# A hybrid RWKV-7 and expert layer: an early gathered tile of 128 prompt tokens, and 544 instead of 672 tokens through all experts

## The chip, the cores and the metric

The kernel runs on one core of one Trainium2 chip. The metric is the device time of an execution in microseconds; lower is better. Before the change the median of three runs is 3515.53 us.

## The reference, cut to what matters

One layer is computed for 1024 prompt tokens and 32 sample tokens (8 sequences of 4), 1056 tokens in all, with a model width of 1024.

```python
def hybrid_layer(x, p, start_pos, shift_prev, wkv_prev, pool_prev, lw):
    n1 = rmsnorm(x, lw['norm_mix_g'])
    z = n1 @ lw['w_in']
    y_r, shift_new, wkv_new = rwkv7_mix(z[..., :D_SHIFT], ...)      # a scan over time with a matrix state
    y_p, pool_new = pool_mix(z[..., D_SHIFT:], pool_prev, ...)      # windowed means
    h = x + jnp.concatenate([y_r, y_p], axis=-1) @ lw['w_out']
    h = h + peer_ffn(rmsnorm(h, lw['norm_ffn_g']), lw['peer_wq'], lw['peer_keys'], lw['peer_u'], lw['peer_v'])
    gate = jax.nn.sigmoid(rmsnorm(h, lw['norm_ple_g']) @ lw['ple_gate_w'])
    h = h + (p @ lw['ple_w']) * gate
    return h, shift_new, wkv_new, pool_new

def block_fn(xb):                                    # of peer_ffn
    q = (xb @ wq).reshape(PEER_BLOCK, 8, 2, 128)
    s1, s2 = ...                                     # scores against two sets of 128 keys
    v1, i1 = lax.top_k(s1, 16); v2, i2 = lax.top_k(s2, 16)
    sc, ci = lax.top_k(all 256 sums v1 + v2, 16)
    expert = e1 * 128 + e2                           # 8 heads x 16 of 16384 experts per token
    gate = jax.nn.softmax(sc, axis=-1)
    ue = jnp.take(u_tab, expert, axis=0)
    act = gelu(einsum('thkd,td->thk', ue, xb)) * gate
    ve = jnp.take(v_tab, expert, axis=0)
    return einsum('thk,thkd->td', act, ve)
```

Each token so uses 128 of 16384 experts, each with a row of 1024 numbers in u and one in v. The outputs are the normed tokens and the new states, all in float32.

## The kernel before

Activations lie with the features on the 128 partitions and the tokens along the free dimension. Matmul operands are split into a high and a low part (hi, lo), and a product is three matmuls: hi by hi, hi by lo, lo by hi.

The instructions are written by a framework that orders them itself: it plays the program on a timeline, and at each moment an engine takes the ready instruction that stands earliest in the program text. The order within an engine is fixed at build time. Work that stands late in the text so fills gaps early, if its inputs and its memory are there. A pool of tiles (tile_pool) takes its memory when it is opened and gives it back when it is closed. DMAs are issued on the SP queue (nc.sync), the gathers on POOL's.

The stages in the text:

- **Phase A** (phase_a): the projections w_in of all 1056 tokens, the parts of RWKV that need no scan (written to fd), and the windowed means through pool_w (pmm, pdf; result yp_d). Each projection wmm also carries wsplit (L177 to L187): blocks of w_out and wq are loaded, split into hi and lo and stored to wc_d, by pieces of 256 KB, through single buffers sraw, shi and slo. For w_out only the first half of the rows is split.
- **Chunks** (bchunk): the scan over the prompt in 16 chunks of 64 tokens, each dependent on the state of the one before, and one chunk for the samples. The output goes to y_d. BC says which chunks are emitted with which stage.
- **ple and wpool** (L981, L998): p @ ple_w for all tokens, to pl_d; and x plus the pooled half of w_out for all tokens in slices of 352, to hx_d.
- **Phase C** (phase_c, one group of GROUPS at a time): y @ w_out (first half) + hx gives h (hT_d); the norm; 16 blocks of wq give the queries; their products with the keys are the scores (sc_d). Weights come from wc_d (wblock, L641); the last group splits its last blocks itself.
- **top and select** (L753, L772): for 128 tokens, on DVE, the 16 best of each half, of the sums, and the gates.

The experts are computed in two ways. Tokens in [GA, GB) are dense: for them select also writes the gates as one-hot products into g_d (L869 to L884), and all 16384 experts are computed in 128 blocks of 128: ublock (L1077: u, gelu), ugate (L1132: times the gate), vblock (L1145: v, eight ublocks at a time into OT). Each block streams 512 KB (esplit, L1057: eraw is split on ACT into ehi and on DVE into elo; upre does the first NPRE on POOL) and does 48 matmuls in emm (L1075) of ND/2 columns. The other GT tokens are gathered, in tiles of 128 (L1170 on): for each of 128 slots one indirect DMA on POOL (L1179) brings each token's own row of u (512 KB in all) into one of NROW = 4 buffers named row; one DVE instruction multiplies by the token and sums (L1187). After gelu and gate, 128 such gathers of v follow, each added to po on DVE (L1196). po is transposed on PE, added to h and stored in h2_d.

Tail (L1220 on) does the last gate, ple_gate_w, the sum and the final norm, once for the dense tokens (td) and once for the gathered ones (tg).

Lines that the text speaks of: keep and pconst (L106, L111), GROUPS and GA, GB (L40, L41), segs and tiles_of (L672, L678), merge (L919), the loop over steps (L1088 to L1118), the rows pool (L1125).

Of the kernel before, what the change touches and what calls it, by code (L numbers as in the profile page):

```python
# [19 lines left out]
D = 1024  # L20
KB = D // 128
NP = 1024
# [18 lines left out]
GROUPS = ((0, 288), (288, 544), (544, 800), (800, 1056))  # L41
GA, GB = 0, 672
# [19 lines left out]
def body(ctx, tc, io):  # L62
# [12 lines left out]
    hx_d = dram.tile([128, KB, T], F32, name="hx_d")  # L75
# [30 lines left out]
    keep = ctx.enter_context(tc.tile_pool(name="keep", bufs=1))  # L106
# [4 lines left out]
    pconst = phases.enter_context(tc.tile_pool(name="pconst", bufs=1))  # L111
# [8 lines left out]
    pbx = ExitStack()  # L120
# [44 lines left out]
    keys = pconst.tile([128, 2, 128], F32)  # L165
# [288 lines left out]

    maxn = max(b - a for a, b in GROUPS)
    def bchunk(c, sp=None):
# [7 lines left out]
        pos = 0 if smpl else NSMP + 64 * c  # L464
# [83 lines left out]
        def sample_s(k, o, last):  # L548
            for p in range(4):
                apb = sp[0][0].tile([128, NB, m], F32, name="apb", bufs=2)  # L550
# [42 lines left out]
        if smpl:  # L593
            po = out()
            for p in range(4):
                ps = PS(pst)
                for i, (k, s_) in enumerate(((1, vt), (0, u))):
                    uvb = sp_.tile([m, NB, 64], F32, name="uvb", bufs=2)
# [42 lines left out]
    def wblock(gi, b):  # L641
# [4 lines left out]
        for i in range(1 if b < KB else 2):  # L646
# [25 lines left out]
    def segs(gi):  # L672
        c0, c1 = GROUPS[gi]
        if c0 == 0:
            return ((0, NP, NSMP), (NSMP, 0, c1 - NSMP))
        return ((0, c0 - NSMP, c1 - c0),)
# [5 lines left out]
    def phase_c(gi):  # L682
# [14 lines left out]
        for k in range(HK):  # L697
            split(k, y[:, k, :n], yhi, ylo)
# [73 lines left out]
    def select(tk, col, m, V12, I12):  # L772
# [133 lines left out]

    def t_stream(gi):
        for t0, m in tiles_of(gi):
            if GA <= GROUPS[gi][0] + t0 < GB:
                yield from top(tk, GROUPS[gi][0] + t0, m)  # L910

    def t_len(gi):
        n = 0
        for t0, m in tiles_of(gi):
            if GA <= GROUPS[gi][0] + t0 < GB:
                n += 24 + m // 4
        return n
# [11 lines left out]
    BC = (0, 2, 4, 8, 12, 16)  # L929
# [23 lines left out]
    with tc.tile_pool(name="smp", bufs=1) as sp_, tc.tile_pool(name="hx", bufs=1) as hx:  # L953
# [17 lines left out]
        pT = sp_.tile([128, 2, T], F32, name="pT")  # L971
        nc.sync.dma_start(pT, io["p"])

        def split(pool, raw, shape, nm, bufs):
            hi = pool.tile(shape, F32R, name=nm + "hi", bufs=bufs)
            ACT(hi, raw, AF.Copy)
            lo = pool.tile(shape, F32R, name=nm + "lo", bufs=bufs)
            TT(lo, raw, hi.bitcast(F32), op=ALU.subtract)
            return hi, lo

        def ple():  # L981
            phi, plo = split(sp_, pT, [128, 2, T], "p", 1)
            for db in range(KB):
                wp = sp_.tile([128, 2, 128], F32, name="wp", bufs=2)
                nc.sync.dma_start(wp, io["ple_w"][db])
                hi, lo = split(sp_, wp, [128, 2, 128], "w", 2)
                pss = [PS("b3"), PS("b3"), PS("b2")]
                for k in range(2):
                    for w, x, first, last in ((hi, phi, k == 0, False), (hi, plo, False, False), (lo, phi, False, k == 1)):
                        for i, ps in enumerate(pss):  # L990
                            mm(ps[:, :XW], w[:, k, :], x[:, k, i * XW:(i + 1) * XW], start=first, stop=last)
                for i, ps in enumerate(pss):
                    o = sp_.tile([128, XW], F32, name="pout", bufs=2)
                    ACT(o, ps[:, :XW], AF.Copy)
                    nc.sync.dma_start(pl_d[:, db, i * XW:(i + 1) * XW], o)
                yield

        def wpool():  # L998
            yhi = hx.tile([128, PB, T], F32R, name="yhi")
            ylo = hx.tile([128, PB, T], F32R, name="ylo")  # L1000
            for g in range(PB):
                raw = hx.tile([128, T], F32, name="yraw", bufs=1)
                nc.sync.dma_start(raw, yp_d[:, g, :])
                ACT(yhi[:, g, :], raw, AF.Copy)
                TT(ylo[:, g, :], raw, yhi[:, g, :].bitcast(F32), op=ALU.subtract)
            for b in range(KB):
                raw = hx.tile([128, HK, 128], F32, name="wraw", bufs=2)
                nc.sync.dma_start(raw, io["w_out"][b, :, HK:, :])
                hi = hx.tile([128, HK, 128], F32R, name="whi", bufs=2)
                ACT(hi, raw, AF.Copy)  # L1010
                lo = hx.tile([128, HK, 128], F32R, name="wlo", bufs=2)
                TT(lo, raw, hi.bitcast(F32), op=ALU.subtract)
                for i in range(T // XW):
                    cs = slice(i * XW, (i + 1) * XW)
                    x = hx.tile([128, XW], F32, name="x", bufs=3)
                    nc.sync.dma_start(x, io["x"][:, b, cs])
                    ps = PS("b2")
# [361 lines left out]
```

## Time and profile before

| | us |
|---|---|
| runs shown | 3515.53, 3530.12, 3499.31 |
| median | 3515.53 |
| the profiled execution's own time | 3494.25 |
| its span, first to last instruction | 3492.4 |
| busy PE / DVE / POOL / ACT | 3262.7 / 2675.0 / 1769.3 / 1179.8 |
| first and last gather issued | 1499.8 and 3317.4 |

A row of a group names line, engine, operation, output and inputs, the shape and the count; behind the bar stand the busy time in us, the mean of one in ns, the idle time of the engine just before them, and what ended it. Consecutive matmuls overlap in the record, so their pace is read from one start to the next, not from the mean. In the windows each engine's busy time stands with its count of instructions in brackets, then the granted clock of TensorE, the DMA engines' busy share and GB/s.

### The profile page before, as it was taken

To read this page: it belongs to the slowest core of one execution; us is meant where nothing else is said; L and a number is where in the kernel's file an instruction comes from. 1 tells how busy PE (TensorE), PEld (TensorE's weight loads), DVE (VectorE), ACT (ScalarE), POOL (GpSimd) and SP (SyncE) were. 2 spreads that over 40 slices of the span, in tenths; PEclk is the share of its full clock that TensorE was granted. 3 is DMA by queue.
4 is the path that set the end of the run, shared out by engine and by line. 5 is a ranking of instruction groups with operands and counts; after the bars stand their busy time and mean duration, and the time that the engine had idled before them with its cause. 6 is when DMAs were issued, how large, how long until landed. Compare 5 with 4: busy or idle time off the path is not lost.

```text
span 3492.4 us, 57600 instructions
## 1 busy us (share of the span) xinstructions
PE 3262.7 (93%) x21831; PEld 3150.6 (90%) x21831; DVE 2675.0 (77%) x5366; ACT 1179.8 (34%) x1776; POOL 1769.3 (51%) x1433
## 2 busy tenths in 40 slices
PE   8997998999999899999999999999999999999997
PEld 7876998989989788999999999999999999999997
DVE  6767333279999799978788778878888787788866
ACT  6452424345556455322122122122122212222243
POOL 5434234145465454156656555555555565555635
PEclk9998999999999899999999999999999999999999
DMA  5667645767767867479888888889898898898834
GB/s 177 213 197 177 185 134 148 213 174 231 210 194 212 282 199 258 131 278 318 308 315 307 306 320 311 313 318 317 314 321 315 307 312 308 301 318 313 311 123 132
DMA packets 467861, 883.61 MB, mean 253 GB/s; under 512 B 129280, under 2 KB 252416, under 8 KB 463104
## 3 DMA queue, kind: packets, MB, share of 16 engines
q1 hardware_dynamic: 356992, 477.24, 43.5%
q0 software_dynamic: 110592, 402.70, 32.6%
q8 instruction: 171, 2.80, 0.3%
q14 instruction: 106, 0.87, 0.1%
HBM read 759.22 MB, written 120.60 MB: 252 GB/s over the span
## 4 chain that ended last, share of the span: by engine, by line
DMA 26%; PE 22%; DVE 19%; issue 14%; POOL 11%; ACT 1%; SPq 0%; POOLq 0%; DVEq 0%; ACTq 0%
DMA row<-v,idx 14%; POOL row L1179 10%; DMA row<-u,idx 7%; PE pd L1075 7%; PE ps L881 2%; DVE ab L875 2%; PE ps L663 2%; PE ps L661 2%; DVE row L1187 2%; PE ps L662 2%; DVE elo L1063 1%; DVE po L1196 1%; PE ps L526 1%; DVE ab L877 1%; DMA sraw<-wq 1%
## 5 line engine op out<-in xcount | busy, mean ns | idle before, releaser
L1179 POOL DMA_INDIRECT row<-u,idx x384 | 534.9, 1393 | 387.9 <-DVE row L1187 248.4
L1179 POOL DMA_INDIRECT row<-v,idx x384 | 520.5, 1355 | 377.3 <-DVE po L1196 222.4
L1196 DVE SCALAR_TENSOR_TENSOR po<-row,act,po 128x1024 f32<-128x1024 f32 x381 | 488.8, 1283 | 152.6 <-DMA row<-v,idx 147.8
L1187 DVE SCALAR_TENSOR_TENSOR row<-row,xt 128x1024 f32<-128x1024 f32 x384 | 463.6, 1222 | 179.4 <-DMA row<-u,idx 177.8
L1075 PE MATMUL pd<-XH,elo 128*128 128x336 f32 x2176 | 524.9, 323 | 52.2 <-DVE elo L1063 49.3
L1061 ACT ACTIVATE ehi<-eraw 128x1024 fp32r<-128x1024 f32 x278 | 293.0, 1054 | 750.3 <-PE pd L1075 676.1
L1075 PE MATMUL pd<-wh,elo 128*128 128x336 f32 (+1 forms) x2112 | 509.5, 320 | 31.2 <-DVE elo L1063 30.9
L1075 PE MATMUL pd<-XH,ehi 128*128 128x336 f32 x2176 | 518.0, 319 | 4.1 <-DVE OT L1150 2.3
L1075 PE MATMUL pd<-XL,ehi 128*128 128x336 f32 x2176 | 519.5, 320 | 0.0
L1075 PE MATMUL pd<-wh,ehi 128*128 128x336 f32 (+1 forms) x2112 | 506.5, 319 | 8.7 <-DVE tg L1260 6.3
L1075 PE MATMUL pd<-wl,ehi 128*128 128x336 f32 (+1 forms) x2112 | 504.3, 318 | 0.0
L1075 PEld LDWEIGHTS pd<-XH,elo 128*128 128x128 f32 x2176 | 376.9, 191 | 64.4 <-DVE elo L1063 61.5
L1075 PEld LDWEIGHTS pd<-wh,elo 128*128 128x128 f32 x2112 | 362.1, 189 | 40.1 <-DVE elo L1063 39.4
L1075 PEld LDWEIGHTS pd<-XH,ehi 128*128 128x128 f32 x2176 | 377.7, 192 | 5.1 <-ACT wt L1081 2.5
L1075 PEld LDWEIGHTS pd<-XL,ehi 128*128 128x128 f32 x2176 | 376.7, 191 | 0.2
L1075 PEld LDWEIGHTS pd<-wh,ehi 128*128 128x128 f32 x2112 | 364.2, 189 | 10.5 <-issue 8.4
L1075 PEld LDWEIGHTS pd<-wl,ehi 128*128 128x128 f32 x2112 | 364.3, 189 | 0.0
L1063 DVE TENSOR_TENSOR elo<-eraw,ehi 128x1024 fp32r<-128x1024 f32 x257 | 317.9, 1237 | 11.7 <-ACT ehi L1061 6.3
L1140 ACT ACTIVATE wh<-wt 128x672 fp32r<-128x672 f32 x128 | 97.5, 766 | 662.1 <-DVE wt L1138 662.1
L881 PE MATMUL ps<-ab 128*128 128x128 f16 x1344 | 195.9, 295 | 25.0 <-DVE ab L877 12.0
L124 POOL TENSOR_TENSOR ab<-ab,e 128x512 f16<-128x512 f16 x110 | 128.4, 1169 | 172.2 <-DVE ab L877 130.7
L882 ACT ACTIVATE gst<-ps 128x512 f32<-128x512 f32 x168 | 179.5, 1103 | 94.4 <-PE ps L881 92.5
(499 smaller groups left out, 5962.7 us busy)
## 6 DMA issues: line engine op xcount, KB each, us to landing
eraw<-uT SPq DMA_DIRECT2D x128, 512.0 KB, 5.4
eraw<-vP SPq DMA_DIRECT2D x128, 512.0 KB, 5.7
g_d<-gst SPq DMA_DIRECT2D x21, 2048.0 KB, 8.4
gq<-g_d SPq DMA_DIRECT2D x32, 1344.0 KB, 9.4
whi<-wc_d SPq DMA_DIRECT2D x148, 256.0 KB, 4.4
wlo<-wc_d SPq DMA_DIRECT2D x148, 256.0 KB, 4.7
wc_d<-shi SPq DMA_DIRECT2D x40, 256.0 KB, 2.6
wc_d<-slo SPq DMA_DIRECT2D x40, 256.0 KB, 3.1
```

Of the source, the lines that this page charges most:

```text
L124: nc.gpsimd.tensor_tensor(out, a, b, op=op)
L661: mm(ps[:, :n], whi[:, kk, :], xhi[:, k, :n], start=k == 0, stop=False)
L662: mm(ps[:, :n], whi[:, kk, :], xlo[:, k, :n], start=False, stop=False)
L881: mm(ps[:, i * 128:(i + 1) * 128], ab[:, k, :, i], ab[:, 0, :, i], start=k == 2, stop=k == 1)
L882: ACT(st[:, :, t2:t2 + 4].rearrange("p e t -> p t e"), v3(ps, 128), AF.Copy, scale=1.0 / GS)
L1061: ACT(hi, raw, AF.Copy)
L1063: sub(lo, raw, hi.bitcast(F32), op=ALU.subtract)
L1075: mm(ps[:, a, :n], w_[:, k, :], x_[:, s:s + n], start=first, stop=last)
L1140: ACT(wh, wt_, AF.Copy)
L1179: nc.gpsimd.indirect_dma_start(out=r[:m], out_offset=None, in_=io[tab], in_offset=bass.IndirectOffsetOnAxis(ap=idx[:m, hh, k:k + 1], axis=0))
L1187: STT(r[:m], r[:m], 1.0, xt[:m], op0=ALU.mult, op1=ALU.mult, accum_out=pre[:m, k:k + 1])
L1196: STT(po[:m], r[:m], act[:m, k:k + 1], po[:m], op0=ALU.mult, op1=ALU.add)
```

## The change

- The last 128 places of the token order become the first 128 prompt tokens (NE = 128; position() maps them). They are a group of their own, the first one, and are gathered. The dense part shrinks from 672 to 544 tokens, the gathered part grows from 384 to 512: four tiles instead of three. The input p is laid out in the new order.
- Phase C of this group stands alone behind phase A; its top runs in the stage of the sample chunk, ple and chunks 2 to 5. The pool rows and the pool keep are opened before, so that gathers need not wait for the memory of the phases. In the loop over the tiles this tile comes first.
- wpool and hx_d are removed: phase C multiplies both halves of w_out, with the rows yp_d and x loaded for each group; wsplit so splits both halves.
- The chunks move: BC is (0, 2, 6, 10, 14, 16). The last step merges phase C of the last group with the first dense blocks.
- Buffers are cut to make room: gst two to one, ab three to two, apb and uvb two to one, NPRE seven to six; ple and the tail of the gathered tokens use tiles of other pools.

```diff
-GROUPS = ((0, 288), (288, 544), (544, 800), (800, 1056))
-GA, GB = 0, 672
+NE = 128
+GROUPS = ((T - NE, T), (0, 288), (288, 544), (544, 800), (800, T - NE))
+GA, GB = 0, 544
...
-        for i in range(0, HK if b < KB else KB, HK):
+        for i in range(0, KB, HK):
...
+    def position(t):
+        return t + T - NE if t < NE else t - NE + NSMP
...
-        y = work.tile([128, 4, maxn], F32, name="y", tag="yp")
-        nc.sync.dma_start(y[:, :, :n], y_d[:, :, c0:c1])
-        for d, s, L in segs(gi):
-            nc.sync.dma_start(h[:, :, d:d + L], hx_d[:, :, s:s + L])
+        for part in range(2):
+            y = work.tile([128, 4, maxn], F32, name="y", tag="yp")
+            if part:
+                for d, s, L in segs(gi):
+                    nc.sync.dma_start(y[:, :, d:d + L], yp_d[:, :, s:s + L])
+                    nc.sync.dma_start(h[:, :, d:d + L], io["x"][:, :, s:s + L])
+            else:
+                nc.sync.dma_start(y[:, :, :n], y_d[:, :, c0:c1])
...
-            st = gp.tile([128, EB, TC], F32, name="gst", bufs=2)
+            st = gp.tile([128, EB, TC], F32, name="gst", bufs=1)
...
-                ab = gp.tile([128, 3, EB, 4], F16, name="ab", bufs=3)
+                ab = gp.tile([128, 3, EB, 4], F16, name="ab", bufs=2)
...
-    BC = (0, 2, 4, 8, 12, 16)
+    BC = (0, 2, 6, 10, 14, 16)
...
+    keep = ctx.enter_context(tc.tile_pool(name="keep", bufs=1, reuse_waits="tile"))
+    rows = ctx.enter_context(tc.tile_pool(name="rows", bufs=1, reuse_waits="tile"))
+    ws = phases.enter_context(tc.tile_pool(name="ws", bufs=2, reuse_waits="tile"))
...
+    for _ in phase_c(0):
+        pass
...
-        merge([(30, bchunk(-1, ((sp_, ssm), bmask, cmask, spads))), (b_len(*BC[1:3]), b_stream(*BC[1:3]))])
-        for st in (ple(), wpool()):
-            for _ in st:
-                pass
+        merge([(60, bchunk(-1, ((sp_, ssm), bmask, cmask, spads))), (b_len(*BC[1:3]), b_stream(*BC[1:3])), (KB + 1, ple()), (t_len(0), t_stream(0))])
...
-    NPRE = 7
+    NPRE = 6
...
-    for step in range(1, NG + 1):
+    for gi in range(1, NG):
+        streams = [(24, phase_c(gi))]
+        if gi > 1:
+            streams.append((t_len(gi - 1), t_stream(gi - 1)))
+        if gi < NG - 1:
+            c_ = BC[gi + 1:gi + 3]
+            streams.append((b_len(*c_), b_stream(*c_)))
...
+            for _ in streams.pop()[1]:
+                pass
+            gstack.close()
+            gqp = ctx.enter_context(tc.tile_pool(name="gqp", bufs=2, side="right", reuse_waits="tile"))
+            streams.append((NPRE, upre()))
+        merge(streams)
+    for pos in range(GB, T - NE, 128):
+        for _ in top(tk, pos, 128):
+            pass
...
-    for col in range(0, GT, 128):
-        m = min(128, GT - col)
+    for col in (GT - NE, *range(0, GT - NE, 128)):
+        m = 128
...
-    GH = gh.tile([128, KB, GT], F32)
-    nc.sync.dma_start(GH, h2_d)
+    GH = []
+    for i in range(KB // 2):
+        GH.append(rows.tile([128, 2, GT], F32, name="GH", tag="row", bufs=NROW))
+        nc.sync.dma_start(GH[-1], h2_d[:, 2 * i:2 * i + 2, :])
```

More of the change, by code (lines that the diff above doesn't have):

```diff
@@ L645, in wblock @@
         out = []
-        for i in range(1 if b < KB else 2):
+        for i in range(2):
             ks = slice(i * HK, (i + 1) * HK)
@@ L991, in ple @@
                             mm(ps[:, :XW], w[:, k, :], x[:, k, i * XW:(i + 1) * XW], start=first, stop=last)
+                o = work.tile([128, 4, maxn], F32, name="pout", tag="yp").rearrange("p a b -> p (a b)")[:, :T]
                 for i, ps in enumerate(pss):
-                    o = sp_.tile([128, XW], F32, name="pout", bufs=2)
-                    ACT(o, ps[:, :XW], AF.Copy)
-                    nc.sync.dma_start(pl_d[:, db, i * XW:(i + 1) * XW], o)
+                    ACT(o[:, i * XW:(i + 1) * XW], ps[:, :XW], AF.Copy)
+                nc.sync.dma_start(pl_d[:, db, :], o)
                 yield
[L998 to L1017, printed above, removed]
-                    mm3(ps, [(hi, lo)], (yhi[:, :, cs], ylo[:, :, cs]), XW)
-                    TT(x, ps[:, :XW], x, op=ALU.add)
-                    nc.sync.dma_start(hx_d[:, b, cs], x)
-                    yield
         spads = (sp_.tile([128, 4, 4, 64], F32, name="spd"), sp_.tile([64, 4, 4, 64], F32, name="slp"))
@@ L1267, in gates @@
                     self.more = [self.tmp()]
-                    ACT(self.more[0], self.src[:, db, :], AF.Square)
+                    ACT(self.more[0], self.src(db), AF.Square)
         def finish(self):
```

110 lines of the change are left out of this document (42 added, 68 removed).

## The prediction

> **What bounds the kernel now.** I read the page first, then the windows by stage, then the two groups of gathers.
>
> ```profile
> span 3492.4 us, 57600 instructions
> 600.00:800.00 200.00, 190.66 (x1514) 184.69 (x1513) 101.09 (x445) 80.68 (x163) 63.77 (x73) 0.97 0.69 202
> 800.00:1000.00 200.00, 188.27 (x1547) 182.30 (x1545) 193.19 (x741) 112.92 (x178) 111.87 (x105) 0.97 0.73 202
> 1000.00:1200.00 200.00, 185.41 (x1536) 175.76 (x1535) 188.23 (x729) 112.88 (x182) 96.70 (x101) 0.98 0.78 234
> 1200.00:1300.00 100.00, 90.01 (x598) 83.80 (x599) 86.70 (x316) 53.30 (x75) 62.55 (x58) 0.88 0.69 217
> 1300.00:1400.00 100.00, 91.93 (x716) 86.32 (x714) 92.06 (x351) 51.20 (x68) 44.85 (x40) 0.97 0.81 265
> 1400.00:1500.00 100.00, 97.38 (x620) 97.11 (x621) 96.24 (x495) 33.48 (x48) 20.48 (x33) 0.98 0.37 115
> 1600.00:3200.00 1600.00, 1520.55 (x9677) 1501.68 (x9676) 1289.45 (x1544) 351.11 (x429) 924.30 (x673) 0.99 0.89 313
> ```
>
> Columns: stretch, length, busy time (and count) of PE, weight load, DVE, ACT and POOL, granted clock, DMA share, GB/s. From 800 to 1500 us PE and DVE are both above nine tenths busy: the lists of experts and the one-hot gates go through DVE while PE does phase C. From 1600 on PE is 95% busy with the dense experts and the DMA engines 89%. PE alone looks like the bound of that stage. The gather rows say otherwise:
>
> ```profile
> L1179 POOL DMA_INDIRECT row<-u,idx x384: 932/1567/2445, 1499.8 to 3282.4; - x192
> L1179 POOL DMA_INDIRECT row<-v,idx x384: 932/1312/1992, 1537.9 to 3317.4; - x192
> DMA to landing us min/median/max: 4.2/6.2/11.8
> ...
> L1179 POOL DMA_INDIRECT row<-u,idx x384 | 534.9, 1393 | 387.9 <-DVE row L1187 248.4
> L1179 POOL DMA_INDIRECT row<-v,idx x384 | 520.5, 1355 | 377.3 <-DVE po L1196 222.4
> L1196 DVE SCALAR_TENSOR_TENSOR po<-row,act,po 128x1024 f32<-128x1024 f32 x381 | 488.8, 1283 | 152.6 <-DMA row<-v,idx 147.8
> L1187 DVE SCALAR_TENSOR_TENSOR row<-row,xt 128x1024 f32<-128x1024 f32 x384 | 463.6, 1222 | 179.4 <-DMA row<-u,idx 177.8
> L1075 PE MATMUL pd<-XH,elo 128*128 128x336 f32 x2176 | 524.9, 323 | 52.2 <-DVE elo L1063 49.3
> L1075 PE MATMUL pd<-wh,elo 128*128 128x336 f32 (+1 forms) x2112 | 509.5, 320 | 31.2 <-DVE elo L1063 30.9
> ```
>
> 768 gathers run without a break from 1499.8 to 3317.4 us: 2.37 us each, call it 2.38 with the pauses between tiles. They have four row buffers, so one buffer turns in 4 x 2.38 = 9.5 us. Of that 6.2 us (median) is issue to landing, 1.25 us is the DVE instruction, and the rest is waiting for DVE and POOL. So the gather is a loop limited by latency: DVE waits 325.6 us in all for landing rows (177.8 + 147.8), 0.42 us a gather, and what PE loses, it loses because the weight split (elo) stands behind such a wait on DVE: 80.2 us. Dense and gather end nearly together. Making the dense part shorter alone therefore doesn't end the stage sooner; three tiles of gathers still need it.
>
> **The change, part by part.** First the dense matmuls, 336 columns before and 272 after:
>
> ```profile
> 2440.87 0.47 PE L1075 MATMUL pd<-wh,elo 128*128 128x336 f32 x2
> 2441.18 0.46 PE L1075 MATMUL pd<-wh,ehi 128*128 128x336 f32 x2
> ...
> 700.35 0.30 PE L663 MATMUL ps<-hi,wlo 128*128 128x288 f32 x1
> 700.49 0.29 PE L661 MATMUL ps<-hi,whi 128*128 128x288 f32 x1
> ...
> 390.86 0.89 PE ps L583 x8
> 391.76 0.89 PE ps L588 x8
> ```
>
> Start to start, two matmuls of 336 columns take 0.307 us (averaged over the neighbours), 153.3 ns each; at 288 columns it is 133.3 ns. That is 0.417 ns a column above 13.3 ns. 272 columns then give 126.7 ns. The eights of 64 columns (0.89 us) show a floor of 112 ns, under which no 128x128 weight goes; 126.7 lies above it. In the dense stage a matmul really takes 1600/9677 = 165.3 ns, 1.078 of the pitch; with the same factor 272 columns take 136.6 ns. Left at the start of the dense stage are 250 of 256 blocks (48 matmuls each) and 384 matmuls of gates: 12384 x 0.1366 = 1692 us. PE gets some 330 us shorter, all of it beside the gathers.
>
> Phase C has five groups of tokens (128, 288, 256, 256, 128) where it had four (288, three of 256), and each does the pooled half of w_out itself. Before: 480 matmuls a group, 480 x (133.3 + 3 x 120) = 237 us, and the removed pass wpool, 288 of 352 columns at 160 ns, 46 us. After: 576 x (112 + 133.3 + 120 + 120 + 112) = 344 us. The two groups of 128 tokens sit on the floor of 112 ns. That is +61 us.
>
> ```profile
> L881 PE MATMUL ps<-ab 128*128 128x128 f16 x1344 | 195.9, 295 | 25.0 <-DVE ab L877 12.0 <-DVE ab L878 4.4 <-ACT gst L882 3.6
> L875 DVE TENSOR_TENSOR ab<-iota,e 128x1024 f16<-128x1024 f16 x168 | 147.2, 885 | 23.8 <-PE ps L881 21.9 <-POOL ab L124 1.2
> L877 DVE TENSOR_TENSOR ab<-ab,e 128x512 f16<-128x512 f16 x168 | 91.0, 551 | 0.3
> L878 DVE TENSOR_TENSOR ab<-ab,e 128x512 f16<-128x512 f16 x58 | 35.2, 607 | 0.2
> ```
>
> 128 tokens fewer need a one-hot: 32 of 168 steps, 37 us of PE (195.9 x 32/168) and 52 us of DVE (273.4 x 32/168). The dense blocks done ahead go from seven of 336 columns to six of 272: 336 x 0.1533 - 288 x 0.1267 = 15 us less. Net for PE before the dense stage: +61 - 37 - 15 = +9 us. The one gate buffer instead of two (gst) makes each 32 tokens wait for a 2 MB store; I cost it at nothing, since phase C and the chunks stand beside it on PE; uncovered it would be up to 17 stores.
>
> In phase A each of the first eight weight blocks is now split in two pieces:
>
> ```profile
> 233.44 4.01 DMA sraw<-wq
> ...
> 290.23 3.43 DMA sraw<-wq
> 293.72 0.71 issue
> 294.46 1.28 POOL slo L124
> 295.76 0.32 SPq L187
> 296.18 3.27 DMA sraw<-wq
> ...
> 301.79 1.75 POOL pads L948
> ...
> ACT shi L183 <- DMA sraw<-wq: 69.6, 13, 20.2
> ```
>
> This is the chain that ended last: load, ACT, POOL, store, next load, through single buffers, 6.0 us a piece (296.18 - 290.23), and 7.1 in the mean from 233.44 to 290.23, eight pieces. It is on the chain from 233 us to the clearing of the chunk pads at 302 us. Eight more pieces cost 8 x 7.1 = 57 us if all show and nothing if the new order hides them. I take 25, near the middle.
>
> Now the early tile. It adds 256 gathers to 768, on POOL (1.37 us each), DVE and DMA.
>
> ```profile
> whi<-wc_d SPq DMA_DIRECT2D x148, 256.0 KB, 4.4
> ...
> 350.65 2.68 DMA yp_d<-zv
> ...
> L767 DVE FIND_INDEX8 I<-V,s 128x8 uint32<-128x128 f32 x128 | 35.4, 283 | 0.0
> ```
>
> Phase C of the first 128 tokens can start when the pooled rows are stored, about 355 us. Its 48 weight pairs are 25 MB; with three pairs in flight and 4.4 us a piece that is some 72 us. Its expert lists follow; the row shows one of five like passes, 35.4 us for the whole kernel, so the five cost a tile about 20 us and the selection, I estimate, as much again: 45 us of DVE. First gather at about 650 us (560 to 700). From 600 to 1500 DVE is idle for 98.9 + 6.8 + 11.8 + 13.3 + 7.9 + 3.8 = 142.5 us. To that come 52 (one-hot) and 45 (this tile's lists are done before); a quarter of the first 98.9 lies before 650 and drops out. That leaves 215 us. A gather takes 1.29 us of DVE (1.222 and 1.283, and the read of the accumulator), so 167 of 256 fit in by 1500 us; 89 are left, I take 85, between none and 256. POOL has room (63.8 to 111.9 busy of 200). DMA has less: 134 MB of rows and 80 more weight pairs (228 for 148), 42 MB, into stretches of 0.69 to 0.81.
>
> Then the sum, on the profile's own times. The full gather loop starts at 1500 + 25 = 1525 us with 768 + 85 = 853 to go, at 2.38 us: the same four buffers, and the weights now come faster (0.5 MB in 6.56 us instead of 7.93), so I expect no shorter landing; 2.30 to 2.50 are the bounds. Dense ends at 1400 + 25 + 9 + 1692 = 3126 us. Until then (3126 - 1525)/2.38 = 673 are done. 180 remain, without the dense part beside them: between POOL's 1.37 + 0.3 = 1.67 us and 2.38; I take 1.75, near POOL's, since the shortest landing, 4.2 us, would give less. 180 x 1.75 = 315, so the gathers end at 3441 us.
>
> The Trainium skill ("DMA: Bandwidth & Descriptors", Anatomy of one DMA — SWDGE (gpsimd) path) fits one such transfer as about 2.0 us and its bytes over 436 GB/s, an estimated 3.2 us for 512 KB. The trace has 4.2 at the least and 6.2 in the median beside the weights; by the page the last 180 would run at POOL's pace, and the sum would be 14 us shorter.
>
> ```profile
> L1196 DVE SCALAR_TENSOR_TENSOR po<-row,act,po x381: 1272/1284/1346, 1550.7 to 3323.8; 128x1024 f32<-128x1024 f32 x191
> ```
>
> Behind the last gather lie 167 us today (3325 to 3492). The dense tokens' gates, 384 x 0.1533 = 59 us, move ahead of it, and the other gates grow from 384 to 512 columns, 192 matmuls x 53 ns = 10 us: 118 us. The dense tail's other splits and the four smaller loads of GH I cost at nothing beside these. Span 3441 + 118 = 3559; 1.85 us lie around the span (3494.25 against 3492.4), so 3561. The profiled execution is the fastest of those shown; the median is 1.0061 of it. 3561 x 1.0061 = 3583 us, about 1.9% slower. I say 3580.
>
> **The rivals.**
>
> *The early tile fits (faster).* All 256 gathers are issued before 1500 us and phase A hides its pieces. For it: the loop would have time, 850/2.38 = 357 gathers; DVE is half idle before 800 us, and the next group's lists come only after it. Against it: 256 x 1.29 = 330 us of DVE where I count 215. Then the loop starts at 1500 with 768; dense ends at 3101; 95 remain: 3101 + 166 + 118 = 3385, in the median 3408. The point from which it decides: the end equals today's when (3374 - 3126)/1.75 = 142 remain at 3126, that is 47 left over, so from 209 early gathers on it is faster.
>
> *The gathers stall the early stage.* DVE takes its instructions in order; a row that lands late holds the masks, lists and one-hots behind it, and PE and POOL wait for those. Price: 0.42 us for each of 167 gathers, 71 us onto the way to the dense stage. 3559 + 71 = 3630, in the median 3654. For it: the same happens in the dense stage, where PE loses 80 us. Against: there DVE often has little else, and low-priority work is placed in gaps. The Trainium skill ("TensorE: Matmul & The Clock Gate", Architectural detail) calls DVE's queue strictly first in, first out; the trace agrees by the 80.2 us that PE waits for elo.
>
> *The early tile isn't early.* If its gathers find no place before the dense stage, 1024 start at 1525: 351 remain at 3126, 614 us more, 3126 + 614 + 118 = 3858, in the median 3884. For it: they stand last in the program. Against: today's gathers stand behind the whole dense loop too and start as soon as their lists and memory are there.
>
> **How the numbers follow.** Forecast 0.47 (own range 3500 to 3670), early tile fits 0.28, stalls 0.15, not early 0.10. A measurement of this kernel tells about 1% from no change (its three runs span 3499 to 3530). Faster by over 1%: nearly all of the second case and the forecast's lowest edge, 0.29. Within 1%: 0.15 of the forecast and 0.02 of the second, 0.17. Slower: 0.54. The range 3380 to 3760 holds the forecast, the stalls and two thirds of the second case; the last case and the second's lower part are left out.
>
> **What would show it.** Right: gather instructions from about 650 us, some 150 to 200 of them before the first tile of the old kind; DVE above nine tenths from 700 to 1500; a dense pitch near 137 ns; dense done near 3130 while gathers go on alone until about 3440, at under 2 us each; 2.3 to 2.5 us a gather before that; the split chain of phase A 25 us longer. Wrong: all 256 before 1500, or a gather in the dense stage well under 2.3 us, either of which makes it faster; PE idle between 700 and 1400 beyond its present few per cent speaks for the stalls; no gather before 1400 for the last.

## The result: 8.3% slower, and the profile after

| | before | after |
|---|---|---|
| median of the runs on one chip, us | 3519.87 | 3811.12 |
| lowest and highest, us | 3499.31, 3530.12 | 3794.56, 3815.26 |
| ratio of the times, 95% interval | 1 | 1.0827 (1.0767 to 1.0886) |
| span of the profiled execution, us | 3492.4 | 3813.4 |
| first gated dense block (first wl), us | 1404 | 1860 |
| last v block of the dense part (OT), us | 3370 | 3432 |
| last gather issued, us | 3317 | 3667 |

The forecast was 3580 us, with a range from 3380 to 3760. The kernel got slower, as forecast, but by 8.3% and not by 1.9%. The windows of the changed kernel, with the columns that the prediction names:

```profile
600.00:800.00 200.00, 158.93 (x1130) 149.97 (x1128) 139.52 (x326) 72.42 (x151) 126.13 (x116) 0.86 0.84 240
800.00:1000.00 200.00, 182.40 (x1474) 175.22 (x1473) 130.25 (x222) 74.22 (x146) 122.95 (x101) 0.99 1.01 296
1000.00:1200.00 200.00, 160.70 (x1135) 148.69 (x1133) 183.54 (x630) 75.08 (x138) 132.23 (x130) 0.84 0.91 296
1200.00:1400.00 200.00, 128.70 (x881) 118.71 (x879) 180.10 (x606) 63.17 (x91) 128.08 (x102) 0.76 0.84 277
1400.00:1600.00 200.00, 116.98 (x757) 104.37 (x756) 186.69 (x563) 65.23 (x98) 132.30 (x116) 0.73 0.85 286
1600.00:1800.00 200.00, 146.01 (x845) 135.00 (x844) 187.80 (x710) 66.21 (x105) 100.75 (x116) 0.59 0.82 267
1900.00:3400.00 1500.00, 1460.32 (x11486) 1449.54 (x11485) 1258.85 (x1631) 396.03 (x512) 848.14 (x613) 1.00 0.90 321
3450.00:3650.00 200.00, 0.00 (x0) 0.00 (x0) 132.81 (x164) 2.15 (x5) 129.92 (x105) 0.50 0.83 279
```

Before, PE was over nine tenths busy from 600 to 1500 us. Now it is busy 117 to 161 of 200 us between 1000 and 1800, DVE over nine tenths, and the granted clock falls to 0.59. From 800 to 1000 the DMA engines are full (1.01). The early stage has become long: it is there that the time went. The dense stage itself is as foreseen or better.

The first rows are the gathers of the line that issues them, in the windows 0 to 1500, 1860 to 3432 and 3432 to 3700 us; behind them the first and last gated block, and the five stores of h by phase C:

```profile
L1156 POOL DMA_INDIRECT row<-u,idx x112: 932/973/2845, 632.3 to 1458.0; - x112
L1156 POOL DMA_INDIRECT row<-v,idx x106: 932/975/4221, 691.1 to 1497.0; - x106
...
L1156 POOL DMA_INDIRECT row<-v,idx x317: 932/1180/2314, 1866.2 to 3413.8; - x159
L1156 POOL DMA_INDIRECT row<-u,idx x310: 932/1467/2317, 1902.9 to 3431.3; - x155
...
L1156 POOL DMA_INDIRECT row<-v,idx x64: 932/978/1994, 3455.2 to 3666.7; - x64
L1156 POOL DMA_INDIRECT row<-u,idx x59: 932/1058/1972, 3431.3 to 3636.1; - x59
...
L1119 DVE TENSOR_TENSOR wl<-wt,wh x128: 700/718/1292, 1860.2 to 3378.1; 128x544 fp32r<-128x544 f32 x128
...
L717 SPq DMA_DIRECT2D hT_d<-h x5: 550/561/561, 475.4 to 1733.2; - x5
```

218 gathers are issued before 1500 us, and 275 before the first gated block. The early tile does get in early. But the last group's h is stored at 1733 us where it was stored at 1269. That store lies a third of the way through the group's phase C, behind the 8 blocks of w_out and ahead of the 16 of wq:

```profile
L710 SPq DMA_DIRECT2D hT_d<-h x4: 523/552/557, 584.7 to 1268.7; - x4
...
L1142 DVE TENSOR_TENSOR wl<-wt,wh x128: 831/852/1398, 1404.0 to 3317.0; 128x672 fp32r<-128x672 f32 x128
```

(These two are the kernel before.) What stands in the way between 1000 and 1820 us is seen in the chain of work that ended last, where the 2 MB stores of the one-hot gates now lie on the path:

```profile
by line: DMA g_d<-gst 9.4%; DVE row L1164 8.2%; DVE ab L882 7.9%; issue 6.4%; DVE po L1173 5.7%; DVE ab L884 4.9%; PE ps L888 3.8%; DVE I L770 2.7%; PE pd L1059 2.2%; DVE s L772 2.1%; PE ps L666 2.1%; DVE V L769 2.1%; DVE ab L885 2.1%; ACT 
...
1342.17 12.39 DMA g_d<-gst
1379.37 17.89 DMA g_d<-gst
1623.88 16.32 DMA g_d<-gst
```

Before, the same store took 8.4 us in the median, and none is among the longest pieces of the chain from 1000 us on:

```profile
DMA to landing us min/median/max: 7.6/8.4/13.6
```

So three things are in view at once: slow stores, DVE full, and POOL with gathers in its order. The experiments take them apart.

### The profile page after: what moved, and what is told of

Read it like the earlier page. It is cut to its first block, busy times and chain, and to the rows that moved or that the text cites. A ratio compares the mean times of both kernels' runs of the same rounds, so it can differ in the third digit from the quotient of the medians.

```text
span 3813.4 us, 59645 instructions
## 1 busy us (share of the span) xinstructions
PE 3120.8 (82%) x22262; PEld 2971.9 (78%) x22262; DVE 2904.6 (76%) x5664; ACT 1142.0 (30%) x1811; POOL 2094.8 (55%) x1714
## 4 chain that ended last, share of the span: by engine, by line
DMA 24%; PE 22%; DVE 22%; issue 15%; POOL 14%; ACT 3%; SPq 1%; POOLq 0%; DVEq 0%; ACTq 0%
DMA row<-v,idx 12%; POOL row L1156 10%; PE pd L1059 8%; DMA row<-u,idx 4%; DVE po L1173 4%; DVE row L1164 3%; DMA g_d<-gst 2%; DMA sraw<-wq 2%; PE ps L666 2%; PE ps L664 2%; DVE ab L882 2%; PE ps L665 2%; POOL slo L123 1%; DVE ab L884 1%; DVE elo L1047 1%
## 5 line engine op out<-in xcount | busy, mean ns | idle before, releaser
L1164 DVE SCALAR_TENSOR_TENSOR row<-row,xt 128x1024 f32<-128x1024 f32 x512 | 658.0, 1293 | 202.0 <-DMA row<-u,idx 199.9
L1059 PE MATMUL pd<-XH,elo 128*128 128x272 f32 x2176 | 457.3, 292 | 28.2 <-DVE elo L1047 22.5
L1059 PE MATMUL pd<-XH,ehi 128*128 128x272 f32 x2176 | 456.1, 291 | 16.6 <-DVE wt L1237 7.1
L1059 PE MATMUL pd<-wh,elo 128*128 128x272 f32 (+1 forms) x2112 | 453.1, 293 | 13.2 <-DVE elo L1047 12.9
L1059 PE MATMUL pd<-wh,ehi 128*128 128x272 f32 (+1 forms) x2112 | 451.6, 293 | 8.9 <-DVE wt L1237 4.7
L1059 PE MATMUL pd<-XL,ehi 128*128 128x272 f32 x2176 | 453.4, 290 | 0.0
L1059 PE MATMUL pd<-wl,ehi 128*128 128x272 f32 (+1 forms) x2112 | 452.1, 293 | 0.0
L664 PE MATMUL ps<-hi,whi 128*128 128x256 f32 (+2 forms) x912 | 310.3, 343 | 16.5 <-DMA whi<-wc_d 8.8
L666 PE MATMUL ps<-hi,wlo 128*128 128x256 f32 (+2 forms) x912 | 305.4, 336 | 4.1 <-DMA wlo<-wc_d 3.6
L665 PE MATMUL ps<-lo,whi 128*128 128x256 f32 (+2 forms) x912 | 300.8, 331 | 4.5 <-POOL lo L123 4.2
```

The lines of the kernel that those rows point to most:

```text
L664: mm(ps[:, :n], whi[:, kk, :], xhi[:, k, :n], start=k == 0, stop=False)
L665: mm(ps[:, :n], whi[:, kk, :], xlo[:, k, :n], start=False, stop=False)
L666: l = mm(ps[:, :n], wlo[:, kk, :], xhi[:, k, :n], start=False, stop=k == K - 1)
L1059: mm(ps[:, a, :n], w_[:, k, :], x_[:, s:s + n], start=first, stop=last)
L1164: STT(r[:m], r[:m], 1.0, xt[:m], op0=ALU.mult, op1=ALU.mult, accum_out=pre[:m, k:k + 1])
```

## The experiments

The medians stand with the ratio to the kernel before on the same chip. "Start" is the first gated block, the first start in the row of wl; that is where the early stage ends. Start, last OT and last gather are of one profiled execution each. The four runs of e11 lie 39 us apart, so a difference of 20 or 30 us between two kernels is near the noise.

| kernel | median, us | ratio (95%) | start | last OT | last gather |
|---|---|---|---|---|---|
| after | 3811.12 | 1.0827 (1.0767 to 1.0886) | 1860 | 3432 | 3667 |
| e1, no early rows | 3529.98 | 1.0040 (1.0020 to 1.0061) | 1578 | 3150 | 3383 |
| e2, early rows held back | 4037.96 | 1.1492 (1.1417 to 1.1568) | 1575 | 3149 | 3894 |
| e4, split alone | 3916.27 | 1.1146 (1.1072 to 1.1220) | 1382 | 2940 | 3778 |
| e5, small buffers alone | 3579.38 | 1.0187 (1.0121 to 1.0253) | 1498 | 3455 | 3352 |
| e6, more pieces alone | 3552.35 | 1.0110 (1.0074 to 1.0145) | 1429 | 3430 | 3378 |
| e7, five row buffers | 3375.00 | 0.9612 (0.9591 to 0.9632) | 1411 | 3249 | 3198 |
| e8, split, eight row buffers | 3636.62 | 1.0355 (1.0327 to 1.0382) | 1382 | 2910 | 3501 |
| e10, early rows, thin DVE | 3762.95 | 1.0714 (1.0662 to 1.0767) | 1820 | 3391 | 3629 |
| e11, early DVE alone | 3641.99 | 1.0352 (1.0297 to 1.0406) | 1695 | 3262 | 3492 |
| e12, early rows thin | 3753.35 | 1.0661 (1.0622 to 1.0700) | 1805 | 3372 | 3606 |
| e13, early rows by plain loads | 3730.96 | 1.0594 (1.0554 to 1.0635) | 1798 | 3364 | 3603 |

### What do the early rows cost? e1 and e2

e1 is the changed kernel without the rows of its first tile; e2 has them, but behind the last one-hot step of POOL.

```diff
 (e1)
+        if col == GT - NE:
+            nc.vector.memset(po, 0.0)
-        for hh in range(HEADS):
+        for hh in range(0 if col == GT - NE else HEADS):
 (e2)
+            with tc.issue_after(lastp[0].ins):     # POOL's last one-hot step
                 nc.gpsimd.indirect_dma_start(out=r[:m], ...
```

> The changed kernel without the 256 gathers of the early tile and the 256 DVE instructions that use them (that tile's expert part is left out); everything else stays. Theory A (the gathers take DVE from the one-hots before the dense stage): the dense stage starts near 1450 us instead of 1800, and the whole takes about 3430 us (768 gathers at 2.4 us from 1500, then 110). Theory B (the extra group of 128 tokens, worked first, pushes the other groups and their one-hots back) and theory C (one gate buffer and two one-hot buffers make each 32 tokens wait for a store): the dense stage still starts after 1650 us and the whole takes 3600 us or more.

> The changed kernel with every gather ordered on POOL behind the last one-hot instruction, so that no gather runs in the early stage. Theory A: dense stage from about 1450 us, all 1024 gathers from then on, 3850 us, no gain and no loss against the changed kernel because the gathers cost at the end what they cost at the front. Theories B and C: the early stage stays as long as it is, dense from 1700 us or later, and 4050 us or more.

The first three rows are of e1: gated blocks, stores of h, and the time of the gate stores from issue to landing. The last one is of e2: a window in which gathers run alone.

```profile
L1119 DVE TENSOR_TENSOR wl<-wt,wh x128: 704/718/1261, 1577.8 to 3095.0; 128x544 fp32r<-128x544 f32 x128
...
L717 SPq DMA_DIRECT2D hT_d<-h x5: 560/563/1231, 472.4 to 1449.0; - x5
...
DMA to landing us min/median/max: 9.3/9.7/12.0
```

```profile
3200.00:3880.00 680.00, 1.97 (x8) 1.57 (x8) 447.70 (x543) 3.66 (x12) 431.25 (x353) 0.50 0.82 274
```

Without the early rows the start moves from 1860 to 1578: they cost 282 us of the early stage, and the same 281 us of the whole (3811 against 3530). Put at the end instead, they cost 508 us (4038 against 3530): 256 more gathers, part of them beside the dense stage, the rest alone at 680/353 = 1.93 us. So gathering early is worth 227 us against gathering late. It is not free, which the forecast took it to be. The other 174 us of the later start (1578 against 1404) are there without any early row. Both theories of the expectations so hold a part: the rows, and the rest of the change. The 282 us are the price in a kernel whose gate buffer is cut to one; no run has early rows and two gate buffers, so it stays open how much of the price hangs on that cut.

### The split, the buffers, the pieces: e4, e5, e6

```diff
 (e4: the kernel before, with keep and pconst opened as in the changed one)
-GA, GB = 0, 672
+GA, GB = 0, 544
 (e5: the kernel before, with gst 1, ab 2, apb 1, uvb 1, NPRE 6)
-            st = gp.tile([128, EB, TC], F32, name="gst", bufs=2)
+            st = gp.tile([128, EB, TC], F32, name="gst", bufs=1)
...
 (e6: the kernel before, with both halves of w_out split)
-        for i in range(0, HK if b < KB else KB, HK):
+        for i in range(0, KB, HK):
```

> The kernel before with the split alone moved to 544 and 512 tokens, all four gathered tiles late; group order, chunks and buffers as before (only two small pools change place). Dense from about 1390 us. 1024 gathers from 1480: 660 until dense ends near 3060, the other 360 at 1.9 us, then 120: about 3870 us if the gather loop is what ends the kernel (my loop account). If the loop runs faster beside a shorter dense part, 3600 or less.

> The kernel before with the cut buffers alone: gate buffer one for two, one-hot buffers two for three, apb and uvb one for two, six blocks ahead for seven. Theory C: 21 stores of 8 us or more show, 100 us or more slower, the last one-hot later than 1500 us. Theories A and B: within 40 us of before.

> The kernel before, with both halves of w_out split in phase A (eight pieces more; the stored second half isn't used). If the chain of single buffers sets the end of phase A, the last store comes at about 330 + 8 x 7.1 = 387 us and the whole takes about 3570 us. If the order hides the pieces, within 15 us of before.

e4's gathers alone, behind its dense part, and the first gated blocks of e5 and e6:

```profile
3000.00:3700.00 700.00, 1.97 (x8) 1.57 (x8) 462.10 (x564) 2.59 (x12) 447.54 (x366) 0.50 0.82 276
```

```profile
L1142 DVE TENSOR_TENSOR wl<-wt,wh x128: 833/851/860, 1497.6 to 3399.4; 128x672 fp32r<-128x672 f32 x128
...
ACT gst L882 <- DMA g_d<-gst: 32.4, 12, 7.8
```

```profile
L1142 DVE TENSOR_TENSOR wl<-wt,wh x128: 834/854/1391, 1428.7 to 3373.5; 128x672 fp32r<-128x672 f32 x128
```

The split alone is the worst part: dense ends at 2940, 430 us sooner, and 1024 gathers end at 3778, 461 us later. The whole is 402 us longer (3916 against 3514). The row loop is the bound, and the split feeds it a third more. The rest of the change brings back 105 us of these (3916 to 3811).

The small buffers alone move the start by 94 us, from 1404 to 1498, with 12 waits of ACT for a gate store (32.4 us); the whole gets 65 us longer. Five buffers are cut at once, and no run takes them one by one. The prediction costed the gate buffer at nothing and did not cost the one-hot buffers. The pieces move the start by 25 us, the value the prediction took, and the whole by 41.

The two can't simply be added to 119 of the 174 us, since they lengthen different things. The start waits for two chains. One is phase C up to its last matmul: behind it the dense blocks get the memory for wh and wl (the pools are closed and opened in this order in the text). The other is the gates up to their last store, which the blocks read back. Before, they end at 1397 and 1372 us. In e5 phase C ends at 1372, no later than before, and the last gate store is issued at 1479: the buffers lengthen the gates alone. In e6 both are some 25 us later (1422 and 1398). In e1 both are late, 1571 and 1557. So of phase C's 174 us e6 accounts for 25 and e5 for none; the other 149 were not taken apart. The group of 128 tokens ahead of the others, the doubled w_out in each group and the new order of the chunks are in them, and the clock is (last section).

### Is the loop limited by its buffers? e7 and e8

```diff
 (e7: the kernel before; NPRE makes room)
-    NPRE = 7
+    NPRE = 6
-    NROW = 4
+    NROW = 5
 (e8: e4 with eight)
-    NROW = 4
+    NROW = 8
```

> The kernel before with five row buffers for four (and six blocks ahead for seven, for the room). If the gather is a loop limited by its buffers: 2.38 x 4/5 = 1.90 us a gather, the last one near 2970 us, fewer waits of PE behind rows on DVE, the dense part then ends near 3300, whole about 3440 us. If DMA contention or DVE sets the rate, 2.3 us a gather and 3515 us as before.

> The kernel before with the split at 544 and 512 tokens, all four tiles late, and eight row buffers for four. By the loop account the buffers no longer bind, and DVE does: 1024 x 1.29 + 128 x 4.6 us of dense work = 1910 us from about 1480, 3390 plus 120: about 3520 us, some 400 less than with four buffers. If the rate is set by DMA, about 3900 us, as with four.

Of e7 the dense window and DVE's two groups; then a window beside the dense part, first of e4 and then of e8, and one of e8's gathers alone:

```profile
1600.00:3100.00 1500.00, 1500.00 (x9785) 1499.97 (x9784) 1304.74 (x1566) 363.49 (x433) 946.69 (x679) 1.00 0.93 337
...
L1196 DVE SCALAR_TENSOR_TENSOR po<-row,act,po 128x1024 f32<-128x1024 f32 x381 | 488.6, 1282 | 25.6 <-DMA row<-v,idx 17.6 <-issue 1.5
L1187 DVE SCALAR_TENSOR_TENSOR row<-row,xt 128x1024 f32<-128x1024 f32 x384 | 459.2, 1221 | 64.7 <-DMA row<-u,idx 63.7
```

```profile
1600.00:2800.00 1200.00, 1175.41 (x9301) 1168.27 (x9300) 1003.10 (x1241) 312.66 (x402) 678.07 (x485) 1.00 0.91 325
1600.00:2800.00 1200.00, 1181.35 (x9388) 1178.72 (x9388) 1045.51 (x1289) 318.10 (x403) 702.17 (x518) 1.00 0.93 339
3000.00:3450.00 450.00, 1.97 (x8) 1.57 (x8) 391.76 (x482) 2.16 (x10) 353.54 (x312) 0.50 0.98 366
```

One more buffer takes the gather from 2.38 to 1500/679 = 2.21 us. DVE's waits for landing rows fall from 325.6 to 81.3 us, PE is busy all the window, and the kernel is 3.9% faster than before: 3375 us, the fastest of all here. So four buffers do limit the loop, as the prediction read it, but not alone: a loop that follows its buffers only would have come to 1.90 us, and the gather got 7% faster and not 20%. Eight buffers with the small dense part show the same. Without dense work the gathers go at 450/312 = 1.44 us, where four buffers gave 1.91; beside it they go at 1200/518 = 2.32, where four gave 1200/485 = 2.47, and 1024 of them end too late. The whole, 3637 us, lies between the two expectations. What else holds the loop beside the dense part was not tested; there the DMA engines are at 0.93 and DVE is busy 1046 of 1200 us.

### What in the early rows costs? e10 to e13

Four kernels keep the changed kernel's order of the text and take away parts of the first tile's gathers.

```diff
 (e10: rows fetched, DVE works on 16 columns)
+                w = 16 if col == GT - NE else D
-                STT(r[:m], r[:m], 1.0, xt[:m], ...
+                STT(r[:m, :w], r[:m, :w], 1.0, xt[:m, :w], ...
 (e11: nothing fetched, DVE in full)
-                r = gather("u", hh, k)
+                r = scr if col == GT - NE else gather("u", hh, k)
 (e12: 128 columns fetched, DVE on 896)
+            w = 128 if col == GT - NE else D
+            nc.gpsimd.indirect_dma_start(out=r[:m, :w], out_offset=None, in_=io[tab].rearrange("e (a b) -> (e a) b", b=w), ...
 (e13: as many bytes by SP)
+            if col == GT - NE:
+                i = (hh * TOPK + k) * 128
+                nc.sync.dma_start(r, io[tab][i:i + 128])
+                return r
```

> The changed kernel with the 256 gathers of the early tile in place, but their DVE instructions on 16 columns instead of 1024 (the rest of that tile's sums is left out). If the early gathers cost DVE time before the dense stage: the first gated block at about 1600 us instead of 1860 and the whole near 3560 us. If they cost by their transfers or by holding POOL: still after 1780 and 3730 us or more.

> The first tile's 256 gathers are left out; its 256 DVE instructions over 1024 columns stay and read one tile that is loaded once. The first gated block (wl) starts at 1860 us in the changed kernel, at 1578 without the early tile's rows and at 1820 with the rows and thin DVE instructions. DVE's time is the price: 1780 or later. The transfers or the gathers' order on POOL are the price: 1600 to 1640, since thin DVE instructions gave back 40 us of 282; the whole about 3560, the 3530 of the kernel without early rows and some 30 more.

> The first tile's gathers fetch 128 columns of a row instead of 1024 (64 KB instead of 512 KB a gather, of other rows); the 256 gather instructions on POOL stay, and DVE works on 896 columns. The bytes are the price: the first gated block starts at 1600 to 1680 us and the 2 MB gate stores go back from 17 to 10 us or less. POOL's own time on 256 gathers (1.37 us each, 350 us) is the price: 1760 or later. DVE's time: 1780 or later. If only the wait for the landing on POOL counts, the gathers go in a short time and the start is between, 1650 to 1750.

> The first tile's rows come as plain loads of 512 KB on the SP queue (neighbouring rows, not those that the tokens want); as many bytes into the same four buffers, no gather on POOL. Bytes against each other on the DMA engines are the price: the first gated block still starts at 1780 us or later. The gathers' place on POOL or their packets, one row of 4 KB each, are the price: 1600 to 1680. A third way: the SP queue stands before a row buffer that is not free yet and holds back the loads of weights behind it; then the start is late too, and SP's waits for DVE on row buffers are tens of us.

The last store of h and the first gated block, in the order e10, e11, e12, e13:

```profile
L717 SPq DMA_DIRECT2D hT_d<-h x5: 552/561/1447, 489.9 to 1711.9; - x5
L1119 DVE TENSOR_TENSOR wl<-wt,wh x128: 701/720/1294, 1819.7 to 3337.0; 128x544 fp32r<-128x544 f32 x128
```

```profile
L717 SPq DMA_DIRECT2D hT_d<-h x5: 561/561/564, 468.1 to 1477.9; - x5
L1119 DVE TENSOR_TENSOR wl<-wt,wh x128: 675/719/725, 1695.0 to 3206.2; 128x544 fp32r<-128x544 f32 x128
```

```profile
L717 SPq DMA_DIRECT2D hT_d<-h x5: 549/563/786, 472.7 to 1542.7; - x5
L1119 DVE TENSOR_TENSOR wl<-wt,wh x128: 679/719/729, 1805.4 to 3318.2; 128x544 fp32r<-128x544 f32 x128
```

```profile
L717 SPq DMA_DIRECT2D hT_d<-h x5: 551/561/617, 487.5 to 1674.5; - x5
L1119 DVE TENSOR_TENSOR wl<-wt,wh x128: 700/719/1295, 1798.2 to 3311.0; 128x544 fp32r<-128x544 f32 x128
...
SPq L1158 <- DVE po L1177: 46.3, 37, 3.2
SPq L1158 <- DVE row L1168: 26.0, 21, 3.6
```

| kernel | DVE | gathers on POOL | bytes | last store of h | last matmul of phase C | last gate store | start |
|---|---|---|---|---|---|---|---|
| e1 | no | no | no | 1449 | 1571 | 1557 | 1578 |
| e11 | yes | no | no | 1478 | 1607 | 1672 | 1695 |
| e12 | 7/8 | yes | 1/8 | 1543 | 1686 | 1779 | 1805 |
| e13 | yes | no | yes | 1674 | 1791 | 1748 | 1798 |
| e10 | 1/64 | yes | yes | 1712 | 1814 | 1648 | 1820 |
| after | yes | yes | yes | 1733 | 1855 | 1814 | 1860 |

No theory with a single price stands. For the **start**, e11's 1695 lies between the two expectations and fits neither; e12's 1805 would fit POOL or DVE as the price, e13's 1798 the bytes, and both can't be the only one. Each of the three kernels that leave one part away (e10, e12, e13) keeps 220 to 242 of the 282 us. For the **last store of h** each part has about the same price wherever it is added. DVE costs 29 us (e1 to e11) or 21 (e10 to after); the gathers on POOL 65 (e11 to e12) or 59 (e13 to after); the bytes 196 (e11 to e13) or 190 (e12 to after). For the last matmul of phase C, with which the chain really ends, it is 36 or 40, 79 or 64, and 184 or 169. DVE's part is near the noise; the order of the three is not. In e13 some of the 196 is not bytes against each other: SP stands 46.3 + 26.0 us before row buffers that DVE still uses, and behind it wait the weights. The 190 us from e12 to after, where SP has no part in the rows, are the better number (an eighth of DVE's work is in it too).

The start has a second chain: lists, one-hots and gate stores, on DVE, POOL and PE. The table shows which of the two ends last. In e13, e10 and after the start comes 5 to 7 us behind phase C's last matmul; in e11 and e12 it comes 24 and 27 us behind the last gate store, and phase C has been done for 88 and 120 us. In e1 the two end close together. So e12 without the bytes has phase C back by 169 us, but meets the gates at 1779; e10 without DVE's work has the gates back by 166 us, but phase C still ends at 1814. The early rows load both chains, phase C mostly by their bytes and the gates by DVE (256 x 1.29 = 330 us of instructions stand between the lists), and taking one load off leaves the other. On e12's chain the gate stores take 9.0 to 11.7 us again, about the 10 that its expectation named; but they are issued from 1535 us on, when the early gathers are over.

Why the gates come 107 us later in e12 than in e11, with no more DVE work, stays open. What e12 has more is the 256 gathers on POOL, which also multiplies for the one-hots, and each kernel gets an order of its own; in e12 PE runs at a granted clock of 0.50 in two of the three last hundreds of microseconds before the start.

## Why the prediction was wrong

The sum, by its own terms, on the profiled spans (predicted 3559, measured 3813, 254 apart):

| term | predicted | measured | difference |
|---|---|---|---|
| first gated block (before: 1404) | 1434 | 1860 | +426 |
| from there to the end of dense | 1692 | 1572 | -120 |
| gathers left then | 180 at 1.75 = 315 | 123 at 1.91 = 235 | -80 |
| tail behind the last gather | 118 | 146 | +28 |

(1434 is the prediction's 1400 + 25 + 9; its dense end was 3126.) Of the 426 us in the first row, 282 are the early rows and 144 the rest of the change: e1 starts 174 us after the kernel before, and the prediction had 30 of these. "Slower" was to come from gathers left over at the end of dense work; that term came out smaller than foreseen, and the start decided. So the right direction is in part luck.

- **The loop** was right in the main: before, four buffers at 2.38 us, and e7 is faster with a fifth, though by 7% only. That the split only makes the loop longer is right too: e4. Beside the changed dense stage a gather took 2.51 us (1572 us for 627), where 2.38 was taken and 2.50 the bound; e4 has 2.47.
- **The dense pitch** was 126.7 ns predicted. Two matmuls are 4.00/16 = 0.250 us apart, 125 ns each:

```profile
2439.77 0.41 PE L1059 MATMUL pd<-XH,elo 128*128 128x272 f32 x2
...
2443.77 0.41 PE L1059 MATMUL pd<-XH,ehi 128*128 128x272 f32 x2
```

  In the stage it is 1500/11486 = 130.6 ns, not 136.6: PE waits 33.9 us for elo in these 1500 us, and before it was 68.7 us in 1600, so the factor 1.078 was too large.
- **How many early gathers fit**: 167 foreseen by 1500 us, 218 came, the first at 632 (foreseen: 650). But the count of idle DVE time is not what held them: DVE was to be over nine tenths busy from 700 us on, and from 800 to 1000 it is busy 130 of 200 us, while the DMA engines are full.
- **The step that failed** is the start of the dense stage in the sum, 1400 + 25 + 9, where the early gathers stand at nothing: they were to fill gaps, and the early stage was to keep its length. It was costed at zero in the forecast and at 71 us in the second rival; e1 shows 282. That rival named the right place, and its sign, PE idle between 700 and 1400 us, came true. But its price and its mechanism fell short: it counted only rows that land late before DVE. What the runs show is mostly bytes on the way of phase C (169 to 196 us), and DVE's and POOL's work on the way of the gates. The prediction had read "DMA has less" from a share of 0.69 to 0.81 with 176 MB to come, and then put no number to it. An estimate from its own rows: the idle shares from 600 to 1500 us add up to 273 us, at some 300 GB/s (202/0.69 to 234/0.78) room for 82 MB; the other 94 MB take some 310 us.
- **The gate buffer**, costed at nothing, "uncovered up to 17 stores": e5, with the one-hot buffers cut as well, starts 94 us later, and its gates end 107 us later. Phase C beside them on PE did not hide that: PE is busy 30 of 100 us from 1400 to 1500 there. With the rows in the way the stores that lie on the chain grew from 8.4 to between 12 and 18 us.
- **Phase A's pieces**: 25 taken, 25 measured at the start (e6).
- **Phase C on PE**, +9 net: not measured by itself, but phase C ends 174 us later in e1 than before, and the pieces are 25 of these. The floor is as foreseen, 114 ns (median, 400 to 500 us) for the 128 columns of the first group against 112. But the granted clock, which the sum took as full, is not: the last 384 matmuls of the last group go at 213 ns (median, e1 and after) and take 78 us in the changed kernel, where 112 ns each give 43 (below). That no 128x128 weight goes under 112 ns is too wide: the one-hot matmuls, with f16 weights, are seen down to 94 ns in the kernel before.
- **Gathers alone**: 1.75 us taken as near POOL's pace; 1.91 here, 1.91 in e4, 1.93 in e2. Four buffers still limit it, since with eight it is 1.44 us. POOL's mean of 1.37 us, taken as a floor, was one beside the dense part; alone the median is 0.98 for v and 1.06 for u.
- **The tail**: most of the gates of the dense tokens did not move ahead of the last gather. In the stretch from 3660 us there are three groups like this one, 288 of their 384 matmuls, and PE, idle from 3450 to 3650 us, begins them at a granted clock of 0.55 (3670 to 3690 us):

```profile
L1059 PE MATMUL pd<-XH,elo 128*128 128x272 f32 x96 | 21.3, 305 | 0.3 <-DVE elo L1047 0.3
```

## What to carry to other kernels

Work moved into the gaps of one engine has to be priced on every resource that it takes, bytes first: here a stage whose DMA engines were at 0.7 to 0.8 had no room for 134 MB more in the time, however idle DVE was. Where a stage ends on two chains, look at both ends: taking the load off one shows only as much as the other allows. A loop that turns a few buffers can gain more from another buffer than from moving work, as here (3375 us against 3811); look for the 4 KB per partition first. And a double buffer that covers a store is worth what the store costs once the queue is loaded, not what it costs today.

## What was unexpected of the hardware

**A store beside gathers takes up to twice its time.** The 2 MB gate store takes 8.4 us in the kernel before and 9.7 in e1 (medians). Those on the chain of the changed kernel take 12.4 to 17.9; the others could not be read. The Trainium skill ("DMA: Bandwidth & Descriptors", Queues, rings and completion order) says that an engine serves its queues in turns, packet by packet. A store that shares with one other full queue would then take about double, which is an inference from that page and agrees with the longest of these rows. No run here shows the turns themselves.

**The clock makes a wait longer.** In the changed kernel, after waits of 3.24, 1.21 and 1.89 us within ten, matmuls of 256 columns go at 213 ns and turn to 120 some 3.7 us after PE went on (1486.04 to 1489.7):

```profile
1480.61 1.12 PE L739 MATMUL ps<-ident,h 128*128 128x128 f32 x4 [3.24 <-ACT xt L741]
...
1486.04 0.99 PE L888 MATMUL ps<-ab 128*128 128x128 f16 x7 [1.89 <-POOL ab L123]
1486.78 0.56 PE L664 MATMUL ps<-hi,whi 128*128 128x256 f32 x1
...
1489.06 0.41 PE L665 MATMUL ps<-lo,whi 128*128 128x256 f32 x1
1489.28 0.41 PE L666 MATMUL ps<-hi,wlo 128*128 128x256 f32 x1
...
1490.69 0.28 PE L664 MATMUL ps<-hi,whi 128*128 128x256 f32 x1
1490.81 0.28 PE L665 MATMUL ps<-lo,whi 128*128 128x256 f32 x1
```

The Trainium skill ("TensorE: Matmul & The Clock Gate", The HAM clock gate) gives about 3.4 us of sustained work until the full clock is granted, at half clock before. The trace agrees with these 3.7 us, and with a granted clock of 0.50 where PE stands idle (3450 to 3650 us). It does not agree in the last group of 128 tokens. There PE works from 1788 to 1825 us without a gap that the profile shows, at 213 ns a matmul of 128 columns, and the granted clock stays at 0.50:

```profile
1800.00:1810.00 10.00, 10.00 (x56) 10.00 (x55) 7.77 (x25) 2.43 (x4) 4.10 (x5) 0.50 0.48 142
```

e1 has the same for 38 us, from 1496 to 1535. What keeps the clock down there no run shows.

Counted over phase C's matmuls of 128, 256 and 288 columns from 600 to 1850 us: a step from one start to the next is usually 112, 120 or 133 ns. Steps of 1.35 to 2.2 times that are 794 of 1923 in the changed kernel, 76 us over the usual; 540 of 1931 and 52 us in e1; 224 of 1467 and 19 us before. So at most some 24 of the 282 us of the rows, and some 32 of the other 174, are slow steps at the lower clock; not all of them stand on the way to the start.
